# In the up product's first full pair: banks emptied first, the second pair's differences formed after

## The chip, the core and the metric

The kernel runs on one core of a Trainium2 chip. Five engines work beside each other, each through its own queue in order: TensorE (matmuls, PE in the profile, with its weight loads as PEld), VectorE (DVE), ScalarE (ACT), GpSimd (POOL) and SyncE (SP), which here issues nearly all DMAs. They wait for one another by semaphores. The metric is the device time of one execution in microseconds (us); lower is better. Three runs of the kernel before took 2182.22, 2184.85 and 2186.44 us, median 2184.85.

## What is computed

A decoder trunk of two layers over 1024 positions of width 1024, in float32. Each layer has a mixer (a gated one, then dilated attention) and behind it a dense MLP with a squared ReLU:

```python
for layer in range(DEPTH):
    y = _rms_norm(h, mix_norm_g[layer])
    ...
    h = h + y
    y = _rms_norm(h, mlp_norm_g[layer])
    h = h + jnp.square(jax.nn.relu(y @ w_up[layer])) @ w_down[layer]
return _rms_norm(h, final_norm_g)
```

`w_up` is 1024 x 4096 and `w_down` 4096 x 1024 in each layer. The change lies in the up product, `y @ w_up[layer]`, and so comes twice in a run.

## The kernel before

*Splits.* Every float32 operand of a matmul is split into an upper and a lower part (`split`, L207): ScalarE copies the source to a rounded type (L208), VectorE subtracts that copy from the source (L209). Three matmuls then make one product: upper by upper, upper by lower, lower by upper (`three`, L321).

*Up product by pairs.* The 4096 columns of `w_up` are taken as 16 pairs (q = 0 to 15) of two 128-column tiles; the 1024 positions are two halves. A pair is thus a 2 x 2 block of 128 x 512 results, c11, c21, c12, c22. Pairs 0 and 1 are computed plainly, with 8 products of 4 inputs, while the normed input is still being made. From pair 2 on, the first full pair, a block takes seven products instead of eight (a Strassen-Winograd form): `product` (L326) runs four inputs by three matmuls, 12 matmuls of 128x512, so a full pair has 84. Its order is 1, 5, 6, 7, then 2, 3, 4, the last three accumulated into banks that already hold something:

- bank `a`: product 1, copied by ScalarE to u (L705), later product 2 on top, giving c11
- bank `d`: product 5, copied by ScalarE to c22 (L717), later product 3 on top, for c12 (L745)
- bank `b`: product 6, added by VectorE to u (L727)
- bank `e`: product 7, added by VectorE to c22 (L733), later product 4 on top, for c21 (L750)

So TensorE may begin product 4 only when L733 has read bank e, product 3 when L717 has read bank d, product 2 when L705 has read bank a. L734 then adds u to c22. `squared` (L644) applies ReLU and the square on ScalarE (L646, L647).

*Differences.* The down product takes seven combinations of each pair's four results, so `hidden_terms` (L649) forms four differences on VectorE (L652, L653, L656, L658), and `kept` (L640, L642) stores the seven tiles to memory through SP's queue, 256 KB each. L652 and L658 write to one of two spare buffers, which come free when their stores have landed. Pair 1's differences are formed right after pair 1, as pair 2 begins on TensorE.

*Weights.* While pair q runs, the weights of pair q+1 are prepared: four raw tiles are loaded through SP (L169), GpSimd forms four combinations (L351, L352, L353, L356, in this order, the last three in place), and each of the seven is split. `steps` (L346) is a generator; every `more()` takes one step: the first splits 4 and issues the GpSimd steps 351 to 353, the second splits 1 and issues 356, then 5, 7, 6, 2, 3. In pair 2 the `more()` calls behind product 1 and 5 are placed after ScalarE's copies with `tc.issue_after`, which keeps an instruction of that engine behind a given one in its queue and adds no wait.

*Inputs.* `Terms` holds the inputs of the seven products, four tiles each. `rest` (L420) makes those of product 7 and the first three of product 4 as pair 1 ends; the fourth tile of product 4 is made by `last` (L427) within pair 2: a GpSimd copy (L430), then a split.

*What sets the order.* TensorE's order is the one written. On the other engines a scheduler lists the instructions by when it expects them ready, so the text's order is only a start; `tc.high_priority` and `tc.issue_after` bend it.

## Time and profile before

| | us |
|---|---|
| median of three runs | 2184.85 |
| the profiled execution | 2183.62 |
| its span, first to last instruction | 2180.8 |
| TensorE busy | 2141.2 (98%) |
| VectorE busy | 1548.9 (71%) |
| ScalarE busy | 1087.3 (50%) |
| GpSimd busy | 518.2 (24%) |

The mean granted clock of TensorE is 0.995 of full speed. A profile row of the timeline reads: start in us from the span's start, duration in us, engine, line, operation, output<-inputs by their names without numbers, shape, how many in a row, and in brackets the idle time of the engine before it with what ended it. A row of waits reads: who waited for whom, total us, times, longest. A row of stretches reads: from:to, length, busy time and count of PE, PEld, DVE, ACT and POOL, then the granted clock, the DMA engines' busy share and GB/s. "wp" is a split weight tile, "r" a raw weight tile, "t" a temporary, "b" a spare buffer, "mm" and "at" are PSUM banks, "hid" is the stored hidden tile, "keep" a kept input.

### The profile page before, as it was taken

To read this page: it belongs to the slowest core of one execution; us is meant where nothing else is said; L and a number is where in the kernel's file an instruction comes from. 1 tells how busy PE (TensorE), PEld (TensorE's weight loads), DVE (VectorE), ACT (ScalarE), POOL (GpSimd) and SP (SyncE) were. 2 spreads that over 40 slices of the span, in tenths; PEclk is the share of its full clock that TensorE was granted. 3 is DMA by queue.
4 is the path that set the end of the run, shared out by engine and by line. 5 is a ranking of instruction groups with operands and counts; after the bars stand their busy time and mean duration, and the time that the engine had idled before them with its cause. 6 is when DMAs were issued, how large, how long until landed. Compare 5 with 4: busy or idle time off the path is not lost.

```text
span 2180.8 us, 30391 instructions
## 1 busy us (share of the span) xinstructions
PE 2141.2 (98%) x10360; PEld 1776.6 (81%) x10360; DVE 1548.9 (71%) x2855; ACT 1087.3 (50%) x2200; POOL 518.2 (24%) x372
## 2 busy tenths in 40 slices
PE   9999999999999999999999999999999999999997
PEld 7888887888878888788888887887778888788886
DVE  7875278666688887771357676758976667988867
ACT  7644145555564443351356464656555556544432
POOL 2000224333324323510000000001433332332335
PEclk9999999999999999999999999999999999999999
DMA  6421104444355443333331322221154443554432
GB/s 213 133 70 49 39 27 161 159 156 151 119 181 186 145 151 107 106 123 129 121 76 54 83 56 55 75 55 30 39 179 157 147 155 123 190 169 147 150 91 98
DMA packets 167679, 253.88 MB, mean 116 GB/s; under 512 B 33641, under 2 KB 59364, under 8 KB 167524
## 3 DMA queue, kind: packets, MB, share of 16 engines
q1 hardware_dynamic: 166768, 250.71, 36.2%
q8 instruction: 81, 1.33, 0.3%
q10 hardware_dynamic: 756, 1.23, 0.2%
q14 instruction: 74, 0.61, 0.1%
HBM read 182.50 MB, written 69.37 MB: 115 GB/s over the span
## 4 chain that ended last, share of the span: by engine, by line
PE 78%; DVE 9%; DMA 5%; ACT 4%; issue 2%; POOL 1%; SPq 0%; DVEq 0%; ACTq 0%; POOLq 0%
PE at L180 39%; PE mm L180 37%; PE at L187 1%; DVE wp L209 1%; ACT t L1123 1%; DMA t<-bvec 1%; DMA t<-in_w_dl 1%; DVE y L209 1%; DMA r<-in_w_dn 1%; DMA sc<-st 1%; DVE N L1161 1%; DVE h L308 1%; DVE t L209 0%; DMA h<-in_xT 0%; DMA hr<-hid 0%
## 5 line engine op out<-in xcount | busy, mean ns | idle before, releaser
L208 ACT ACTIVATE wp<-r 128x512 fp32r<-128x512 f32 (+2 forms) x404 | 241.0, 600 | 358.4 <-PE at L180 237.4
L180 PE MATMUL at<-hx,wp 128*128 128x512 f32 x1770 | 413.3, 389 | 1.8 <-DVE h L817 1.7
L180 PE MATMUL mm<-y,whi 128*128 128x512 f32 x1312 | 412.3, 395 | 0.0
L180 PEld LDWEIGHTS at<-hx,wp 128*128 128x128 f32 x1770 | 332.0, 188 | 72.0 <-DVE h L817 3.0
L209 DVE TENSOR_TENSOR wp<-r,wp 128x512 fp32r<-128x512 f32 (+2 forms) x404 | 320.3, 801 | 70.0 <-ACT wp L208 66.4
L180 PE MATMUL at<-t,wp 128*128 128x512 f32 x1344 | 316.1, 391 | 6.3 <-DVE t L733 6.3
L180 PEld LDWEIGHTS at<-t,wp 128*128 128x128 f32 x1344 | 253.6, 189 | 60.0 <-DVE t L733 7.2
L264 POOL TENSOR_TENSOR t<-t 128x512 f32<-128x512 f32 (+1 forms) x66 | 83.6, 1267 | 859.1 <-ACT t L259 857.0
L180 PEld LDWEIGHTS mm<-y,whi 128*128 128x128 f32 x1312 | 240.8, 188 | 50.6
L180 PE MATMUL mm<-y,wlo 128*128 128x512 f32 x656 | 256.0, 390 | 0.0
L351 POOL TENSOR_TENSOR t<-r 128x512 f32<-128x512 f32 (+3 forms) x62 | 93.0, 1500 | 594.2 <-DMA r<-in_w_dn 191.8
L180 PE MATMUL mm<-y,wp 128*128 128x512 f32 x912 | 222.7, 390 | 0.4 <-DVE y L209 0.2
L180 PEld LDWEIGHTS mm<-y,wp 128*128 128x128 f32 x912 | 170.7, 188 | 37.4 <-issue 0.6
L180 PE MATMUL mm<-hx,wp 128*128 128x512 f32 x708 | 172.5, 390 | 2.4 <-DVE hx L209 1.2
L180 PEld LDWEIGHTS mm<-hx,wp 128*128 128x128 f32 x708 | 132.5, 188 | 31.8 <-DVE hx L209 2.0
L180 PEld LDWEIGHTS mm<-y,wlo 128*128 128x128 f32 x656 | 123.2, 188 | 26.6
L209 DVE TENSOR_TENSOR hx<-t,hx 128x512 fp32r<-128x512 f32 x192 | 142.7, 750 | 1.4 <-ACT hx L208 1.4
L817 DVE TENSOR_TENSOR h<-h,at 128x512 f32<-128x512 f32 x144 | 97.9, 682 | 47.7 <-PE at L180 45.7
L209 DVE TENSOR_TENSOR wlo<-r,whi 128x512 fp32r<-128x512 f32 x138 | 99.3, 737 | 41.3 <-ACT whi L208 34.1
L208 ACT ACTIVATE hx<-t 128x512 fp32r<-128x512 f32 x192 | 118.9, 629 | 17.6 <-DMA t<-hid 10.9
L208 ACT ACTIVATE whi<-r 128x512 fp32r<-128x512 f32 x138 | 84.1, 627 | 83.8 <-PE mm L180 54.4
L180 PE MATMUL at<-y,wp 128*128 128x512 f32 x480 | 119.0, 390 | 0.7 <-DVE wp L209 0.7
(199 smaller groups left out, 3211.7 us busy)
## 6 DMA issues: line engine op xcount, KB each, us to landing
t<-hid SPq DMA_DIRECT2D x182, 256.0 KB, 3.1
hid<-t SPq DMA_DIRECT2D x140, 256.0 KB, 2.3
r<-in_w_up SPq DMA_DIRECT2D x128, 256.0 KB, 2.7
r<-in_w_dn SPq DMA_DIRECT2D x88, 256.0 KB, 2.6
hid<-b SPq DMA_DIRECT2D x56, 256.0 KB, 2.1
r<-in_w_qkv SPq DMA_DIRECT2D x50, 256.0 KB, 2.6
r<-in_w_v SPq DMA_DIRECT2D x48, 256.0 KB, 3.1
vd<-vs SPq DMA_DIRECT2D x16, 512.0 KB, 3.9
```

The lines of the kernel that those rows point to most:

```text
L180: nc.tensor.matmul(out, lhsT, rhs, **kw)
L187: nc.tensor.transpose(out, src, ident)
L208: nc.scalar.activation(hi, src, AF.Copy)
L209: nc.vector.tensor_tensor(lo, src, hi.bitcast(F32), op=ALU.subtract)
L264: nc.gpsimd.tensor_tensor(self.acc, self.acc, sq, op=ALU.add)
L308: nc.vector.tensor_tensor(x, x, ps, op=ALU.add)
L351: tt(r3, r[0, 0], r[1, 0], op=ALU.subtract)
L817: return engine.tensor_tensor(hs[i, s], hs[i, s], src, op=ALU.add).ins
L1123: nc.scalar.activation(p[:, c], p[:, c], AF.Exp, bias=m, scale=-1.0, accum_out=dn)
L1161: nc.vector.tensor_tensor(o, o, pv[r, c], op=ALU.add)
```

## The change

```diff
         def last(self):
 
             t4 = temp()
             nc.gpsimd.tensor_copy(t4, self.kept[3][:, 1, :])
-            self.t[4].append(pair("t4").split(t4))
+            return lambda: self.t[4].append(pair("t4").split(t4))
...
+        def held_terms(q):
+            hidden_terms(q, c[q, 0, 0], c[q, 1, 0], c[q, 0, 1], c[q, 1, 1], c[q, 0, 0])
+
...
-                if s and i:
-                    hidden_terms(q, c[q, 0, 0], c[q, 1, 0], c[q, 0, 1], c[q, 1, 1], c[q, 0, 0])
+                if s and i and q == 0:
+                    held_terms(q)
...
             evacuated = nc.scalar.activation(c22, d, AF.Copy).ins
             if q == 2:
                 with tc.issue_after(evacuated):
+                    t4 = x.last()
                     more()
-                    x.last()
...
             b = at_bank()
             product(b, w[6], x.t[6])
-            more()
+            if q > 2:
+                more()
             nc.vector.tensor_tensor(u, u, b, op=ALU.add)
...
             e = at_bank()
             product(e, w[7], x.t[7])
-            more()
-            nc.vector.tensor_tensor(c22, c22, e, op=ALU.add)
+            if q > 2:
+                more()
+            emptied = nc.vector.tensor_tensor(c22, c22, e, op=ALU.add).ins
+            if q == 2:
+
+                with tc.issue_after(evacuated), tc.issue_after(emptied):
+                    t4()
+                    more()
+                    more()
+                    held_terms(1)
             nc.vector.tensor_tensor(c22, c22, u, op=ALU.add)
```

In pair 2 alone, the split of the fourth input tile of product 4, the splits of the next pair's weights 7 and 6, and pair 1's differences with their stores are written behind the addition that empties bank e (L733), and kept behind it in VectorE's queue; the splits among them are kept behind ScalarE's copy of bank d in ScalarE's queue as well. The GpSimd copy for that input tile stays where it was in the text. Pair 0's differences are formed as before. No instruction is added or taken away, and all other pairs are written as before. Line numbers in the prediction are those of the kernel before.

## The prediction

> **What bounds the kernel now.** I read the page first (busy shares and the chain that ended last), then TensorE's waits, then the stretches around the longest of them, then all engines there in order of time. Pairs are the loop's q: pairs 0 and 1 are plain products, pair 2 is the first full one.

> ```profile
> span 2180.8 us, 30391 instructions
> ...
> PE 78%; DVE 9%; DMA 5%; ACT 4%; issue 2%; POOL 1%; SPq 0%; DVEq 0%; ACTq 0%; POOLq 0%
> ```

> ```profile
> PE at L180 <- DVE t L733: 6.3, 2, 4.7
> ```

> ```profile
> 364.84 3.03 PE L180 MATMUL at<-t,wp 128*128 128x512 f32 x12 [1.58 <-DVE t L733]
> ```

> TensorE carries 78% of the chain, so only what makes it wait counts. Its largest wait, 6.3 us in two pieces, is for L733, the addition that empties bank e: twice in the program, once in each layer's MLP (1.58 us in layer 0, 4.74 in layer 1). The stretches price it. Each of the first four runs from product 5 of one full pair to product 5 of the next, and holds the same matmuls.

> ```profile
> 1600.30:1604.30 4.00, 3.96 (x9) 3.13 (x10) 2.48 (x4) 2.75 (x6) 0.00 (x0) 0.50 0.29 90
> ...
> 905.00:908.00 3.00, 3.00 (x7) 2.35 (x8) 3.00 (x6) 0.63 (x1) 1.18 (x2) 0.50 0.48 132
> ...
> 349.50:370.43 20.93, 19.35 (x85) 15.69 (x84) 17.29 (x21) 10.94 (x21) 7.25 (x5) 1.00 0.61 211
> 370.43:389.47 19.04, 19.04 (x85) 15.77 (x84) 15.97 (x20) 11.08 (x21) 7.92 (x6) 1.00 0.57 194
> 1581.84:1607.99 26.15, 21.41 (x85) 17.18 (x84) 22.06 (x29) 14.48 (x27) 8.36 (x6) 0.87 0.61 199
> 1607.99:1627.04 19.05, 19.05 (x86) 15.77 (x85) 14.65 (x18) 10.27 (x18) 8.30 (x6) 1.00 0.51 166
> ```

> The first number is the length, the one before the DMA share the granted clock. Pair 2 costs 20.93 - 19.04 = 1.89 us more than pair 3 in layer 0, and 26.15 - 19.05 = 7.10 us more in layer 1. The latter is a wait of 4.74 us (its row stands below) and 2.36 us of slow matmuls: the clock stood at 0.50 behind it. Together 8.99 us hang on this place. Here is why L733 came late in layer 1:

> ```profile
> 1587.85 0.68 DVE L209 TENSOR_TENSOR wp<-r,wp 128x512 fp32r<-128x512 f32 x1
> 1587.91 0.62 ACT L208 ACTIVATE wp<-r 128x512 fp32r<-128x512 f32 x1
> ...
> 1589.36 1.28 POOL L351 TENSOR_TENSOR t<-r 128x512 f32<-128x512 f32 x1 [7.78 <-DMA hid<-t]
> ...
> 1589.88 1.32 DVE L652 TENSOR_TENSOR b<-t 128x512 f32<-128x512 f32 x1 [1.35 <-DMA hid<-b]
> ...
> 1590.73 1.62 POOL L352 TENSOR_TENSOR r<-r 128x512 f32<-128x512 f32 x1
> 1591.12 1.77 DVE L209 TENSOR_TENSOR wp<-r,wp 128x512 fp32r<-128x512 f32 x1
> ...
> 1592.38 0.64 ACT L208 ACTIVATE wp<-r 128x512 fp32r<-128x512 f32 x1 [1.17 <-POOL r L352]
> 1592.42 1.62 POOL L353 TENSOR_TENSOR r<-r 128x512 f32<-128x512 f32 x1
> ...
> 1592.72 2.88 PE L180 MATMUL at<-y,wp 128*128 128x512 f32 x12
> 1592.82 1.78 DVE L653 TENSOR_TENSOR t<-t 128x512 f32<-128x512 f32 x1
> 1593.99 1.07 POOL L430 COPY t<-keep 128x512 f32<-128x512 f32 x1
> 1594.51 1.09 DVE L209 TENSOR_TENSOR wp<-r,wp 128x512 fp32r<-128x512 f32 x1
> ...
> 1595.03 1.71 POOL L356 TENSOR_TENSOR r<-r 128x512 f32<-128x512 f32 x1
> 1595.10 0.63 ACT L208 ACTIVATE t<-t 128x512 fp32r<-128x512 f32 x1 [2.09 <-POOL t L430]
> 1595.53 1.75 DVE L656 TENSOR_TENSOR t<-t 128x512 f32<-128x512 f32 x1
> ...
> 1597.21 0.68 DVE L209 TENSOR_TENSOR t<-t,t 128x512 fp32r<-128x512 f32 x1
> 1597.81 0.68 DVE L658 TENSOR_TENSOR b<-t 128x512 f32<-128x512 f32 x1
> 1598.41 0.68 DVE L209 TENSOR_TENSOR wp<-t,wp 128x512 fp32r<-128x512 f32 x1
> 1599.01 0.67 DVE L727 TENSOR_TENSOR t<-t,at 128x512 f32<-128x512 f32 x1
> 1599.61 0.68 DVE L733 TENSOR_TENSOR t<-t,at 128x512 f32<-128x512 f32 x1
> ...
> 1600.34 1.22 PE L180 MATMUL at<-t,wp 128*128 128x512 f32 x2 [4.74 <-DVE t L733]
> ```

> VectorE has no gap from 1589.88 on: nine instructions stand ahead of L733, four of them pair 1's differences (L652, L653, L656, L658). Four VectorE subtractions that run beside a POOL instruction take 1.09 to 1.78 us instead of 0.68, and end 0.56 us behind it (1592.82 + 1.78 = 1594.60 against POOL's 1592.42 + 1.62 = 1594.04); POOL's own 1.28 us becomes 1.62. TensorE would have begun product 4 when product 3 ends its 12 matmuls, at 1592.72 + 2.72 = 1595.44 (2.72 being the step between equal products, 19.04/7).

> **The change part by part.** Nothing is added or removed; instructions change places. In the order of the changed program's instructions VectorE has, behind the split at 1587.85: the splits of products 1 and 5's weights, L727, L733, the t4 split, the splits of weights 7 and 6, and only then pair 1's differences, threaded between pair 2's own work. On POOL the t4 copy (L430) moves behind L356. On SP the stores of pair 1's differences move behind two loads.

> *L733.* Weight 1's lower half can follow its upper half at 1587.91 + 0.62 = 1588.53 and end at 1589.2, ahead of POOL's first step (which waits for a store that nothing moves). POOL then runs unheld: 1590.73 + 1.28 = 1592.0. ScalarE's copy of weight 5 takes 0.64, to 1592.65; its subtraction waits out L353 (1592.1 to 1593.4) and ends 0.56 later, 1593.95. L727 and L733 follow in steps of 0.60 (1599.01 to 1599.61): bank e is empty at 1595.2, by 0.25 us in time. The other end: POOL's two steps at 1.62 as now, and 1.78 for each of weight 5's split (from 1593.02), L727 and L733: 1598.2, a wait of 2.8 us. The near end holds, since an addition that reads a bank isn't slowed beside POOL:

> ```profile
> 378.27 0.67 DVE L727 TENSOR_TENSOR t<-t,at 128x512 f32<-128x512 f32 x1
> ```

> ```profile
> 377.88 1.63 POOL L356 TENSOR_TENSOR r<-r 128x512 f32<-128x512 f32 x1 [1.29 <-issue]
> ```

> *t4.* POOL: L356 starts behind weight 5's split, 1593.95 + 1.28 = 1595.2, the copy 1.07 to 1596.3; ScalarE 0.63 to 1596.95, VectorE to 1597.6. Product 4 needs that tile's lower half at its 11th matmul, 1595.44 + 10 x 0.227 = 1597.7. On the edge; with 1.71 for L356, 0.3 us late. I put 0.2 us for L733 and t4 together.

> *What is late next.* Behind the t4 split on VectorE stand ten instructions (weights 7, 6 and 2, L652, L734, L653, L656, L745, L658, weight 3) at 0.60 each, to 1603.6, then pair 2's L652 to 1604.3. SP issues seven stores, the last of them that of this L652, before the third load for pair 4, which feeds L351 and L352:

> ```profile
> 1603.63 0.38 SPq L169 DMA_DIRECT2D r<-in_w_up  x1
> ```

> ```profile
> 1618.88 2.88 PE L180 MATMUL at<-y,wp 128*128 128x512 f32 x12
> ...
> 1621.60 2.88 PE L180 MATMUL at<-t,wp 128*128 128x512 f32 x12
> ```

> ```profile
> r<-in_w_up SPq DMA_DIRECT2D x128, 256.0 KB, 2.7
> ```

> ```profile
> 350.00:355.00 5.00, 5.00 (x24) 4.14 (x23) 3.86 (x6) 3.19 (x6) 1.17 (x1) 1.00 1.00 360
> ```

> That load goes out at 1604.7, 1.1 us later than now, while TensorE comes 7.1 us earlier. Landed after 2.7 us: 1607.4; L351 to 1608.7, L352 (1.62) to 1610.4, ScalarE's weight 5 to 1611.0 and, behind it in ScalarE's queue, pair 3's copy of bank d (0.6) to 1611.6. TensorE needs that copy at product 3, 1618.88 - 7.10 = 1611.78: just in time. L733 of pair 3 stands behind weight 5's subtraction (L353 ends about 1611.8, so 1612.4), L727 and weight 7's (held by L356), and ends near 1615.0 against 1621.60 - 7.10 = 1614.50: 0.5 us. At the full DMA rate of 360 GB/s one 256 KB transfer takes 0.73 us; two stores ahead of the load make it land 1.5 us later, and the wait 2.0 us. The ends are 0 and 2.0; I take 0.5, as the stores are issued about as fast as they drain.

> *Layer 0* has more room.

> ```profile
> 353.83 1.28 POOL L351 TENSOR_TENSOR t<-r 128x512 f32<-128x512 f32 x1 [7.49 <-DMA hid<-t]
> ```

> POOL's L351 comes 353.83 - 349.50 = 4.33 us behind product 5, in layer 1 7.52: every time above has 3.19 us more there, so no wait is left, and the 1.89 us go.

> The sum: -8.99 + 0.2 + 0.5 = -8.3 us. The profiled execution took 2183.62 us (2.8 around its span): 2175.3. The three runs lie at 2182.22 to 2186.44, median 2184.85, from which it would be 2176.5. I predict 2176.0, between the two.

> ```profile
> 904.96 1.56 PE L180 MATMUL mm<-hx,y 128*128 128x512 f32 x3 [2.26 <-DVE b L836]
> ```

> What a leftover wait costs beyond its length: the clock was 0.50 from 905 to 908 (a stretch shown above), right behind this wait of 2.26 us, while the 1.58 us that layer 0 now waits left the clock of its stretch at 1.00. So I charge a wait above some 2 us with 1.5 us more (3 us at half speed). [...]

> **The rivals.**

> *A: the wait shrinks but stays in layer 1's pair 2.* If POOL's and VectorE's blocked durations hold throughout, bank e is empty at 1598.2: 2.8 us of wait and 1.5 of clock come back, with 0.5 later: -8.99 + 4.8 = -4.2, 2180. For: ScalarE's and POOL's steps are chained to a landing store. Against: VectorE is idle from 1589.2 to 1592.65 and no longer holds POOL up.

> *B: the loads of pair 4 come too late; slower.* Place: the third load behind seven stores, in both layers. If it lands x us after 1607.5, layer 1 waits x + 0.5, and layer 0 x - 3.2; above 2 us each pays 1.5 for the clock. At x = 5.1 that is 7.1 + 1.9 = 9.0: all is given back. 5.1 us are seven stores of 0.73, so that is the case of all seven standing in the queues when the load is issued. At x = 6.5, with pair 4's fourth load behind five more stores, it is 8.5 + 4.8 = 13.3, 4.3 above now: 2188. Against: VectorE makes the stores 0.6 us apart or more, so most have drained.

> *C: no change.* The scheduler's order moves a bank's emptying, but the wait only changes its releaser (t4's chain over POOL, 3 us longer than worked): 2183.6. Against: the rows of that chain above.

> **How the numbers follow.** Forecast 0.70 (2173 to 2178.5), A 0.13, C 0.09, B 0.08. The low end is the fastest run less all of 8.99, 2173; the high end, 2181, takes in A. Under 0.2% (4.4 us) this kernel's measurement can't tell from no change: that is 2180.5 to 2189.2. Faster gets the forecast and most of A, 0.81; same takes C and the rest of A, 0.12; slower, from B, 0.07.

> **What would show it.** TensorE's waits: no L733 wait above 0.5 us; both pair-2 stretches at 19.0 to 19.8 us; no clock of 0.50 near 1600. On VectorE L733 ends about 4.4 us earlier after product 5 in layer 1, behind only the three weight splits. L652 to L658 of pair 1 appear in pair 2's second half. Wrong would be: product 4 of pair 2 waiting for the t4 split, or pair 3 waiting more than 2 us, with SP's third load landing after 1609 (on the old clock).

## The result, and the profile after

The changed kernel takes 2176.12 us (median of five runs, 2174.14 to 2177.02) against 2186.44 (five runs, 2182.22 to 2187.48) of the kernel before: a ratio of 0.996, 95% interval 0.995 to 0.9971. In a second comparison it took 2174.65 (five runs, 2172.84 to 2175.51) against 2183.32 (21 runs), ratio 0.996 (0.9947 to 0.9974). The gain is 10.3 us in the first, 8.7 in the second. The profiled execution took 2177.02.

In the changed kernel's lines L705 is L709, L717 is L721, L727 is L732, L733 is L739, L734 is L747, L745 is L758. First its page, the span and the chain's shares:

```profile
span 2174.9 us, 30386 instructions
...
PE 80%; DVE 8%; DMA 5%; ACT 4%; issue 2%; POOL 1%; SPq 1%; DVEq 0%; ACTq 0%; POOLq 0%
```

Then its longest waits of TensorE (who waited for whom, total us, times, longest):

```profile
PE at L187 <- DVE rq L247: 3.4, 3, 2.4
PE mm L180 <- DVE h L308: 3.2, 3, 2.0
```

The wait for the emptying of bank e, 6.3 us and the longest before, has left the list; the two at its head stand at lines that the change doesn't touch. The stretches from product 5 of pair 2 to that of pair 3, and on to pair 4's, in layer 0 (first two rows) and layer 1:

```profile
349.84:368.88 19.04, 19.04 (x85) 15.77 (x84) 13.85 (x22) 11.46 (x22) 6.05 (x5) 1.00 0.60 211
368.88:387.92 19.04, 19.04 (x85) 15.77 (x84) 13.41 (x19) 9.81 (x18) 5.95 (x5) 1.00 0.57 191
1581.04:1600.08 19.04, 19.04 (x85) 15.77 (x84) 14.18 (x23) 11.85 (x23) 6.05 (x5) 1.00 0.52 171
1600.08:1619.45 19.37, 19.37 (x85) 15.69 (x84) 14.01 (x20) 11.52 (x21) 5.84 (x4) 1.00 0.64 216
```

Pair 2 went from 20.93 to 19.04 in layer 0 and from 26.15 to 19.04 in layer 1, at full clock; pair 3 of layer 1 gave back 19.37 - 19.05 = 0.32. So these two places give 1.89 + 7.11 - 0.32 = 8.68 us. All engines in layer 1's pair 2, in order of time:

```profile
1591.31 0.63 ACT L208 ACTIVATE wp<-r 128x512 fp32r<-128x512 f32 x1 [0.87 <-POOL r L352]
1591.36 1.29 POOL L353 TENSOR_TENSOR r<-r 128x512 f32<-128x512 f32 x1
...
1591.98 1.22 DVE L209 TENSOR_TENSOR wp<-r,wp 128x512 fp32r<-128x512 f32 x1 [3.51 <-ACT wp L208]
1592.73 1.63 POOL L356 TENSOR_TENSOR r<-r 128x512 f32<-128x512 f32 x1
1593.12 0.68 DVE L732 TENSOR_TENSOR t<-t,at 128x512 f32<-128x512 f32 x1
...
1593.72 0.67 DVE L739 TENSOR_TENSOR t<-t,at 128x512 f32<-128x512 f32 x1
1594.30 0.61 POOL L430 COPY t<-keep 128x512 f32<-128x512 f32 x1
1594.64 2.88 PE L180 MATMUL at<-t,wp 128*128 128x512 f32 x12
1594.94 0.63 ACT L208 ACTIVATE t<-t 128x512 fp32r<-128x512 f32 x1 [3.00 <-POOL t L430]
1595.61 0.69 DVE L209 TENSOR_TENSOR t<-t,t 128x512 fp32r<-128x512 f32 x1 [1.22 <-ACT t L208]
...
1598.62 0.69 DVE L653 TENSOR_TENSOR t<-t 128x512 f32<-128x512 f32 x1
```

VectorE now idles 3.51 us, then makes weight 5's lower half, L732 and L739 in a row: bank e is empty at 1593.72 + 0.67 = 1594.39, and product 4 starts at 1594.64 with no wait. Pair 1's L653 stands in the second half, where GpSimd has nothing to do, and takes 0.69 us instead of 1.78.

### The profile page after: what moved, and what is told of

It is laid out like the page before. It is cut to its first block, busy times and chain, and to the rows that moved or that the text cites. A ratio compares the mean times of both kernels' runs of the same rounds, so it can differ in the third digit from the quotient of the medians.

```text
span 2174.9 us, 30386 instructions
## 1 busy us (share of the span) xinstructions
PE 2139.6 (98%) x10360; PEld 1774.5 (82%) x10360; DVE 1541.6 (71%) x2855; ACT 1086.5 (50%) x2200; POOL 514.3 (24%) x372
## 4 chain that ended last, share of the span: by engine, by line
PE 80%; DVE 8%; DMA 5%; ACT 4%; issue 2%; POOL 1%; SPq 1%; DVEq 0%; ACTq 0%; POOLq 0%
PE at L180 40%; PE mm L180 39%; PE at L187 1%; DMA t<-bvec 1%; ACT t L1136 1%; DVE wp L209 1%; DMA sc<-st 1%; DMA h<-in_xT 1%; DMA r<-in_w_dn 1%; DMA t<-in_w_dl 1%; DVE N L1174 1%; DMA hr<-hid 1%; DVE h L308 0%; DVE h L830 0%; DVE wlo L209 0%
## 5 line engine op out<-in xcount | busy, mean ns | idle before, releaser
L208 ACT ACTIVATE wp<-r 128x512 fp32r<-128x512 f32 (+2 forms) x404 | 240.9, 600 | 356.4 <-PE at L180 229.0
L180 PE MATMUL at<-hx,wp 128*128 128x512 f32 x1770 | 412.9, 389 | 1.7 <-DVE h L830 1.7
L180 PE MATMUL mm<-y,whi 128*128 128x512 f32 x1312 | 412.4, 395 | 0.0
L180 PEld LDWEIGHTS at<-hx,wp 128*128 128x128 f32 x1770 | 332.0, 188 | 71.7 <-DVE h L830 2.6
L209 DVE TENSOR_TENSOR wp<-r,wp 128x512 fp32r<-128x512 f32 (+2 forms) x404 | 323.5, 808 | 77.2 <-ACT wp L208 73.7
L180 PE MATMUL at<-t,wp 128*128 128x512 f32 x1344 | 313.9, 389 | 0.0
L180 PEld LDWEIGHTS at<-t,wp 128*128 128x128 f32 x1344 | 252.2, 188 | 52.8 <-DVE t L739 0.4
L180 PEld LDWEIGHTS mm<-y,whi 128*128 128x128 f32 x1312 | 240.7, 188 | 50.6
L180 PE MATMUL mm<-y,wlo 128*128 128x512 f32 x656 | 256.0, 390 | 0.0
L351 POOL TENSOR_TENSOR t<-r 128x512 f32<-128x512 f32 (+3 forms) x62 | 92.7, 1494 | 596.6 <-DMA r<-in_w_up 194.1
L180 PE MATMUL mm<-y,wp 128*128 128x512 f32 x912 | 222.7, 390 | 0.4 <-DVE y L209 0.2
L180 PEld LDWEIGHTS mm<-y,wp 128*128 128x128 f32 x912 | 170.7, 188 | 37.4 <-issue 0.6
L180 PE MATMUL mm<-hx,wp 128*128 128x512 f32 x708 | 172.6, 390 | 3.2 <-DVE hx L209 1.6
L180 PEld LDWEIGHTS mm<-hx,wp 128*128 128x128 f32 x708 | 132.4, 188 | 32.9 <-DVE hx L209 2.5
L180 PEld LDWEIGHTS mm<-y,wlo 128*128 128x128 f32 x656 | 123.1, 188 | 26.8
L209 DVE TENSOR_TENSOR hx<-t,hx 128x512 fp32r<-128x512 f32 x192 | 141.1, 741 | 1.9 <-ACT hx L208 1.9
L208 ACT ACTIVATE hx<-t 128x512 fp32r<-128x512 f32 x192 | 119.0, 630 | 17.8 <-DMA t<-hid 13.7
L209 DVE TENSOR_TENSOR wlo<-r,whi 128x512 fp32r<-128x512 f32 x138 | 98.9, 735 | 40.8 <-ACT whi L208 35.6
L208 ACT ACTIVATE whi<-r 128x512 fp32r<-128x512 f32 x138 | 84.0, 627 | 84.4 <-PE mm L180 54.3
L180 PE MATMUL at<-y,wp 128*128 128x512 f32 x480 | 119.0, 390 | 0.7 <-DVE wp L209 0.7
## 6 DMA issues: line engine op xcount, KB each, us to landing
t<-hid SPq DMA_DIRECT2D x182, 256.0 KB, 3.2
hid<-t SPq DMA_DIRECT2D x140, 256.0 KB, 2.3
r<-in_w_up SPq DMA_DIRECT2D x128, 256.0 KB, 2.7
r<-in_w_dn SPq DMA_DIRECT2D x88, 256.0 KB, 2.6
hid<-b SPq DMA_DIRECT2D x56, 256.0 KB, 2.2
r<-in_w_qkv SPq DMA_DIRECT2D x50, 256.0 KB, 2.6
r<-in_w_v SPq DMA_DIRECT2D x48, 256.0 KB, 3.5
```

Of the source, the lines that this page charges most:

```text
L180: nc.tensor.matmul(out, lhsT, rhs, **kw)
L208: nc.scalar.activation(hi, src, AF.Copy)
L209: nc.vector.tensor_tensor(lo, src, hi.bitcast(F32), op=ALU.subtract)
L351: tt(r3, r[0, 0], r[1, 0], op=ALU.subtract)
```

## The experiments

Each starts from the changed kernel; lines shift by a few. "Product 4" and the banks are those of the front; the t4 split is that of the fourth input tile of product 4. Experiments 1 to 3 were timed once each, and 21 single runs of the kernel before lie between 2179.40 and 2187.66 us: what these three show is read from their stretches, not from their times.

**1. The differences alone.** Only pair 1's differences stay behind bank e; the t4 split and the splits of weights 7 and 6 go back to their old places.

```diff
-            return lambda: self.t[4].append(pair("t4").split(t4))
+            self.t[4].append(pair("t4").split(t4))
...
-                    t4 = x.last()
                     more()
+                    x.last()
...
-            if q > 2:
-                more()
+            more()
...
-            if q > 2:
-                more()
+            more()
...
-                    t4()
-                    more()
-                    more()
                     held_terms(1)
```

> Only pair 1's differences are moved behind the emptying of bank e; the t4 split and the splits of weights 7 and 6 stand where they stood before, so VectorE's order is weight 5, the addition from bank b, t4 split, weight 7's split, the addition that empties bank e. Theory (each instruction ahead of that addition costs its place in VectorE's queue, and the t4 split can't start before GpSimd's copy): in the changed kernel the t4 split ran 1595.61 to 1596.30 and weight 7's 1596.22 to 1596.91; the addition would follow to 1597.5 against product 4's place at 1594.64, so TensorE waits 2.9 us in layer 1, with 1.5 to 2.4 us of halved clock behind it: the stretch from product 5 of pair 2 to product 5 of pair 3 takes 23.4 to 24.4 us instead of 19.04. In layer 0, with 2.75 us more room, 0.1 to 0.3 us: 19.1 to 19.4. Rival (the differences are the whole of it, and the splits' place is of no matter): both stretches at 19.04, as in the changed kernel.

2181.59 us, the kernel before beside it 2183.13 (one run each). Waits, stretches (pair 2 of layer 0, then layer 1) and VectorE's rows of layer 1:

```profile
PE at L180 <- DVE t L737: 3.3, 1, 3.3
```

```profile
349.67:368.76 19.09, 19.09 (x85) 15.69 (x84) 13.37 (x21) 10.33 (x19) 6.03 (x5) 1.00 0.55 200
1580.78:1605.03 24.25, 20.94 (x85) 16.84 (x84) 18.03 (x28) 14.70 (x27) 6.42 (x6) 0.93 0.57 195
```

```profile
1593.43 0.67 DVE L731 TENSOR_TENSOR t<-t,at 128x512 f32<-128x512 f32 x1
...
1595.90 0.69 DVE L209 TENSOR_TENSOR t<-t,t 128x512 fp32r<-128x512 f32 x1 [1.80 <-ACT t L208]
...
1597.11 0.68 DVE L737 TENSOR_TENSOR t<-t,at 128x512 f32<-128x512 f32 x1
```

The theory had 23.4 to 24.4 us for layer 1's pair 2 and 19.1 to 19.4 for layer 0's, and 24.25 and 19.09 came; its rival (the differences are all there is, 19.04) falls. With the differences gone, bank b is emptied at 1593.43 (L731), but the t4 split stands ahead of L737 in VectorE's queue, waits 1.80 us for ScalarE, and L737 waits behind it. In layer 0 that is hidden (19.09); in layer 1, 5.2 of the 7.1 us above 19.04 stay.

**2. The splits alone.** The other half: the t4 split and those of weights 7 and 6 stay behind bank e, the differences go back.

```diff
-                if s and i and q == 0:
+                if s and i:
                     held_terms(q)
...
-                    held_terms(1)
```

> Only the t4 split and the splits of weights 7 and 6 are moved behind the emptying of bank e; pair 1's differences stay ahead of it. Theory (place in VectorE's queue): two instructions of 0.60 us less stand ahead than in the kernel before, so the waits of 4.74 and 1.58 us become 3.5 and 0.4: stretches of pair 2 of 24.1 to 25.2 us in layer 1 (3.5 of wait and 1.5 to 2.4 of clock) and 19.4 in layer 0. Rival (the splits, with the t4 copy ahead of them on GpSimd, are the whole of it): both at 19.0 to 19.4.

2179.43 us against 2183.13 (one run each). Waits, stretches and VectorE's rows of layer 1:

```profile
PE at L180 <- DVE t L739: 3.9, 2, 3.7
```

```profile
348.37:367.96 19.59, 19.33 (x85) 15.68 (x84) 16.99 (x21) 10.30 (x19) 7.25 (x5) 1.00 0.63 218
1579.62:1604.22 24.60, 20.95 (x85) 16.83 (x84) 20.98 (x27) 14.37 (x27) 8.35 (x6) 0.93 0.59 203
```

```profile
1593.43 1.75 DVE L656 TENSOR_TENSOR t<-t 128x512 f32<-128x512 f32 x1
...
1596.31 0.68 DVE L739 TENSOR_TENSOR t<-t,at 128x512 f32<-128x512 f32 x1
```

In layer 1 it came as the theory had it (24.1 to 25.2), in layer 0 0.2 us longer than its 19.4: the slowed differences are back ahead of the emptying, and 5.6 us stay in layer 1. There the halves alone give 26.15 - 24.25 = 1.9 and 26.15 - 24.60 = 1.6 us, about a quarter each of the 7.1: either one left ahead of L739 keeps it late, and only both together free it. In layer 0, which had less to lose, the differences alone give 20.93 - 19.09 = 1.84 us of the 1.89 and the splits alone 20.93 - 19.59 = 1.34.

**3. The t4 copy four times over**, to make that chain late by a known amount.

```diff
             t4 = temp()
-            nc.gpsimd.tensor_copy(t4, self.kept[3][:, 1, :])
+            for _ in range(4):
+                nc.gpsimd.tensor_copy(t4, self.kept[3][:, 1, :])
```

> The changed kernel with GpSimd's copy of the t4 tile done four times into the same buffer; nothing else differs, and VectorE's order is the same. The three more copies take 3 x 0.65 us = 1.95 us. Theory (the t4 split was 0.6 us early in layer 1: ended 1596.30, needed by the 11th matmul of product 4 at 1594.64 + 2.27 = 1596.91; 3.4 us early in layer 0): product 4 of pair 2 waits 1.3 us in layer 1, between its 10th and 11th matmul, without loss of clock (under 2 us), and pair 3 loses 0.3 to 1.2 us, as VectorE's queue behind the t4 split is 1.95 us later: stretches 20.3 for pair 2 and 19.4 to 20.3 for pair 3. In layer 0 no wait, 19.04. Rival (the t4 split is not near the edge: the time from GpSimd's copy to product 4 has slack): 19.04 for pair 2 in both layers.

2179.03 us against 2183.13 (one run each). The stretches of pairs 2 and 3 in layer 0, then in layer 1, and TensorE in layer 1:

```profile
349.51:368.55 19.04, 19.04 (x85) 15.78 (x84) 12.08 (x19) 9.75 (x19) 7.89 (x8) 1.00 0.50 168
368.55:388.49 19.94, 19.80 (x85) 15.54 (x84) 13.18 (x19) 10.67 (x20) 5.84 (x4) 1.00 0.62 199
1581.84:1602.14 20.30, 19.58 (x86) 15.70 (x84) 13.71 (x22) 11.38 (x22) 8.04 (x8) 1.00 0.45 154
1602.14:1622.10 19.96, 19.82 (x86) 15.54 (x84) 14.44 (x21) 11.93 (x22) 5.83 (x4) 1.00 0.64 215
```

```profile
1598.13 0.50 PE L180 MATMUL at<-t,wp 128*128 128x512 f32 x1 [0.49 <-ACT t L208]
1598.86 0.72 PE L180 MATMUL at<-t,wp 128*128 128x512 f32 x2 [0.23 <-DVE t L209]
```

Layer 1's pair 2 came as worked out, 20.30. GpSimd's copies took 2.63 us in place of 0.61. Of these 2.02 us, 20.30 - 19.04 = 1.26 reach TensorE, which now waits within product 4 for t4's two halves: the chain had some 0.76 us to spare. The miss is pair 3 of layer 0, 19.94 where 19.04 was expected, from SP's and ScalarE's rows:

```profile
371.23 0.45 SPq L169 DMA_DIRECT2D r<-in_w_up  x1
```

```profile
375.56 0.63 ACT L208 ACTIVATE wp<-r 128x512 fp32r<-128x512 f32 x1 [2.80 <-DMA r<-in_w_up]
...
379.21 0.58 ACT L722 ACTIVATE t<-at 128x512 f32<-128x512 f32 x1
```

The third load of the next pair went out 371.23 - 368.55 = 2.68 us after product 5 and was in use 4.33 us later; in the changed kernel's layer 0 it was 0.74 us (369.62 - 368.88) and 3.02 (to 372.64). So the chain is 1.94 + 1.31 = 3.25 us later here. The expectation had the queue 1.95 us later and nothing for the landing; why the load took longer to land stays open.

**4 and 5. One layer alone.** The new order in layer 0 only (4) and in layer 1 only (5); the edit of 4, with `layer == 0` and `layer != 0` exchanged for those of layer 1 in 5:

```diff
-                if s and i and q == 0:
+                if s and i and (q == 0 or layer != 0):
                     held_terms(q)
...
-                    t4 = x.last()
+                    if layer == 0:
+                        t4 = x.last()
                     more()
+                    if layer != 0:
+                        x.last()()
...
-            if q > 2:
+            if q > 2 or layer != 0:
                 more()
...
-            if q > 2:
+            if q > 2 or layer != 0:
                 more()
...
-            if q == 2:
+            if q == 2 and layer == 0:
```

> The change in layer 0's MLP alone. Theory (the two places add up): pair 2's stretch 19.04 us in layer 0 and some 26 us in layer 1; about 1.9 us faster than before, ratio 0.9991, which five rounds hardly tell from no change. Rival (the gain is somewhere else, or layer 0's share is what the clock makes of it): no change at all, or more than 4 us.

> The change in layer 1's MLP alone. Theory: pair 2's stretch 19.04 in layer 1, 20.9 in layer 0; 7.1 less 0.33 for pair 3, 6.8 us faster, ratio 0.9969. Rival (the extra gain over the 8.7 us of the two places, seen in the medians of the changed kernel, sits in layer 1): 8.5 us or more.

Medians of 11 runs each, beside 2183.32 of the kernel before: layer 0 alone 2181.72, ratio 0.9994 (0.9985 to 1.0002); layer 1 alone 2177.61, ratio 0.9972 (0.9964 to 0.9981). Pair 2 in both layers, of 4 and then of 5:

```profile
349.54:368.58 19.04, 19.04 (x85) 15.77 (x84) 14.31 (x23) 11.59 (x22) 6.12 (x5) 1.00 0.63 214
1578.58:1604.33 25.75, 20.77 (x85) 16.75 (x84) 21.40 (x28) 14.48 (x27) 7.83 (x6) 0.93 0.59 196
```

```profile
349.02:370.04 21.02, 19.34 (x86) 15.69 (x84) 17.31 (x21) 10.94 (x21) 7.24 (x5) 1.00 0.61 208
1581.33:1600.37 19.04, 19.04 (x85) 15.77 (x84) 14.20 (x23) 11.88 (x23) 6.07 (x5) 1.00 0.51 171
```

Each layer's stretch falls to 19.04 where the new order stands and stays near its old length where it doesn't (25.75 against 26.15, 21.02 against 20.93: such a wait varies by some tenths of a us). The medians fall by 1.6 and 5.7 us, where 1.9 and 6.8 were expected; for layer 0 alone the interval holds no change too, so its 1.9 us are shown by the stretch, not by the time. For layer 1 alone it runs from 4.1 to 7.9 us, which holds the 6.8 and not the 8.5 of the rival.

**6. The third load earlier.** Pair 4's weights are requested at high priority, to take the load away from behind the seven stores.

```diff
-            wn = down.weights(0) if down else up_weights(q + 1)
+            with tc.high_priority(offset=PRIO) if q == 3 else nullcontext():
+                wn = down.weights(0) if down else up_weights(q + 1)
```

> The changed kernel, with the loads of pair 4's raw weights at a raised priority, which moves the third of them ahead of five of the seven stores on SP. Theory (pair 3 in layer 1 lost 0.33 us because that load was late for GpSimd's first step, which held ScalarE's copy of bank d): the load goes out near 1599.8 instead of 1603.57, GpSimd's first step starts before 1604 instead of after 1606, and pair 3's stretch is 19.05 instead of 19.37; in time 0.3 us, not to be told from the changed kernel. Rival (VectorE's queue itself is late in pair 3): still 19.3 or more.

2174.69 us (five runs), ratio to before 0.9959 (0.9947 to 0.9972). Pair 3 of layer 1, and GpSimd's first step there:

```profile
1599.64:1618.68 19.04, 19.04 (x85) 15.77 (x84) 16.00 (x22) 12.05 (x22) 6.15 (x4) 1.00 0.70 235
```

```profile
1602.64 1.30 POOL L351 TENSOR_TENSOR t<-r 128x512 f32<-128x512 f32 x1 [8.40 <-DVE b L652]
```

The load goes out behind two stores instead of seven, L351 begins 3.0 us after pair 3's product 5 (1599.64) instead of 6.5 (1606.56 - 1600.08 in the changed kernel), and the pair has no wait left.

**7. The changed kernel again**, beside the runs of 4 to 6.

> The changed kernel once more, beside the others on this chip. Theory (8.99 us less 0.33 at the two places, all else noise): 8.7 us faster than the kernel before, ratio 0.9960. Rival (the 10.3 us between the medians are real and part of it comes from elsewhere): 10 us or more, with stretches outside the two places that are shorter in both profiles of the changed kernel than before.

2174.65 us: the 10.3 us of the first comparison are not repeated, and 8.67 is near what the places add up to (8.68 by the first profile's stretches, 9.00 - 0.04 = 8.96 with this run's pair 3). The interval is 5.7 to 11.6 us, so an agreement to a hundredth is luck. Its pair 3 of layer 1:

```profile
1599.21:1618.30 19.09, 19.09 (x86) 15.71 (x84) 13.63 (x20) 11.19 (x20) 5.81 (x4) 1.00 0.64 215
```

Against 19.04 it lost 0.05 us there, not 0.33, so experiment 6 has nothing left to win, and its time is the same.

## Why the prediction was right

2176.0 was predicted, 2176.12 and 2174.65 were measured. That the first lies within 0.12 us is luck: the kernel before stood at 2186.44 beside it, above both bases of the prediction (2183.62 and 2184.85), and the gain was 10.3 us, not 8.3. The second comparison, with 21 runs of the kernel before and a gain of 8.7, is the fairer test. The steps, one by one:

*8.99 us hang on this place.* Shown by the stretches: pair 2's two lost 9.00 us together, clock included, and each layer's lost its own share when that layer alone was changed (experiments 4, 5).

*L733 (now L739) lies 0.25 us in time.* The prediction's 13.4 us from product 5 to the empty bank (1595.2 - 1581.84) came out at 13.35 (1594.39 - 1581.04), and product 4 began 0.25 us later. (Among the signs to look for, the prediction has L733 some 4.4 us earlier after product 5; its own rows give 1600.29 - 1595.2 = 5.1, and 18.45 - 13.35 = 5.1 came. And the rows that it shows have five slowed subtractions, not four.) The step that mattered was that the additions that read a bank weren't slowed beside GpSimd: L732 and L739 took 0.68 and 0.67, although L356 ran until 1592.73 + 1.63 = 1594.36, while weight 5's subtraction, between two tiles of SBUF, took 1.22 and ended 0.55 us behind L353. Rival A, which had all of them slowed, falls with these rows.

*t4 on the edge, 0.2 us.* It was better: the copy took 0.61 us, not the 1.07 taken from before, where L653, a subtraction between two SBUF tiles, ran beside it until 1594.60; now L739, which reads a bank, was all that did. The lower half was there at 1595.61 + 0.69 = 1596.30, 0.6 us ahead of the 11th matmul (1594.64 + 2.27); experiment 3 gives 0.76 from the other side. The first 0.2 us of the sum was therefore nothing. That t4 could have decided (rival C's mechanism) is true of the place: with the chain 2.02 us later TensorE waits for it.

*0.5 us in pair 3.* The mechanism was right, the size 0.33 and 0.05 us (above 19.04) in the two profiles of the changed kernel. The changed kernel's first profile: SP, then ScalarE, then TensorE's weight loads.

```profile
1598.13 0.33 SPq L642 DMA_DIRECT2D hid<-b  x1
1599.34 2.25 SPq L642 DMA_DIRECT2D hid<-t  x4
1601.74 1.77 SPq L642 DMA_DIRECT2D hid<-b  x2
1603.57 0.44 SPq L169 DMA_DIRECT2D r<-in_w_up  x1
```

```profile
1606.48 0.63 ACT L208 ACTIVATE wp<-r 128x512 fp32r<-128x512 f32 x1 [1.38 <-DMA r<-in_w_up]
...
1610.12 0.58 ACT L721 ACTIVATE t<-at 128x512 f32<-128x512 f32 x1
```

```profile
PEld at L180 <- DVE t L739: 0.4, 1, 0.4
```

The load goes out behind seven stores, 3.49 us after product 5 of pair 3 (3.8 predicted), bank d is copied by 1610.70, 0.26 us ahead of product 3 (1600.08 + 4 x 2.72), and the wait is for L739. Counted from the pair's product 5, the prediction had that copy's end at 10.7 us (1611.6 - 1600.88), with 10.9 allowed. The traces give, for its end and the length of the pair, 7.2 us and 19.04 (experiment 6), 10.4 and 19.09 (7), 10.6 and 19.37 (the first profile), 10.8 and 19.53 (experiment 5), 11.2 and 19.94, 11.3 and 19.96 (experiment 3's layers): from some 10.3 us on, what is late is paid for in full. So B's mechanism is real, but cost half a us at most with the order of the change and 0.9 with its chain made later; the 2 us above which B added a clock charge were not reached.

*Layer 0 has 3.19 us more room.* 2.75 it is (L351 came 7.58 us behind product 5 in layer 1, 4.83 in layer 0); enough, pairs 2 and 3 there are both at 19.04.

*The sum.* The terms should have been -8.99 + 0.05 to 0.33, so -8.7 to -8.9 instead of -8.3; the second comparison has -8.67. The first profiled span fell by less, 5.9 us, because other places moved, which the last section shows in part.

## What to carry to other kernels

A bank's emptying is worth as much as what stands ahead of it in its engine's queue: list those instructions, their producers and their durations beside GpSimd (here up to 1.78 us instead of 0.68), and move behind it all that isn't needed earlier, since each half of the move alone gave a quarter of the layer-1 gain. Then follow what the moved work holds up one stage later: here stores that pushed a load back, which cost 0.05 to 0.5 us, and 0.9 once the moved work itself came 2 us later, because the chain behind that load ends close to when it is needed. Price the place by the whole stretch between equal points, clock included, since the wait alone (4.74 of 7.10 us) undercounts it.

## What the runs showed of the hardware

Whether a wait of some 2 us halves the clock isn't fixed by its length. The prediction charged 1.5 us above about 2 us. One place shows otherwise. In the changed kernel's first profile, TensorE's row that ends a wait (in brackets) and the stretch behind it:

```profile
1509.45 0.73 PE L180 MATMUL mm<-o,whi 128*128 128x512 f32 x2 [1.96 <-DVE h L308]
```

```profile
1510.60:1514.00 3.40, 3.40 (x10) 2.62 (x9) 3.27 (x4) 1.92 (x4) 2.90 (x2) 0.50 0.00 0
```

The same in the kernel before:

```profile
1510.87 0.73 PE L180 MATMUL mm<-o,whi 128*128 128x512 f32 x2 [1.95 <-DVE h L308]
```

```profile
1510.90:1514.30 3.40, 3.40 (x15) 2.82 (x16) 3.37 (x5) 2.03 (x4) 2.01 (x2) 1.00 0.00 0
```

The granted clock is the third number from the end: after 1.96 us it was 0.50, after 1.95 us 1.00. The changed kernel ran 10 matmuls there in the time of the 15 before, 1.1 us lost in work that the change doesn't touch; another 0.5 went to a wait in layer 1's down product (1.41 us against 0.92). That is more than half of the 2.8 us by which the first profiled span fell short of 8.68; the rest stays open. The wait in the down product is no accident of one run: it takes 1.41 to 1.81 us in the five profiles with the whole new order in layer 1, and 0.92 to 1.15 in the other four. What links it to the change stays open. At the place of 905 us that the prediction showed, where 2.26 us had halved the clock, 2.35 us lowered it to 0.50 in the first profile of the changed kernel (from 903.05 to 906.46), and 2.23 left it at 1.00 in the second.

```profile
1507.21:1510.62 3.41, 1.45 (x8) 1.03 (x7) 3.31 (x7) 1.19 (x2) 0.00 (x0) 1.00 0.22 77
```

The wait of 1.95 us before (1508.92 to 1510.87) is cut by a window's edge, and TensorE is busy for 2.56 and 1.74 us in the two windows that share it:

```profile
1505.78:1509.19 3.41, 2.56 (x12) 1.92 (x12) 3.28 (x6) 1.61 (x4) 0.00 (x0) 1.00 0.62 181
1509.19:1512.60 3.41, 1.74 (x8) 1.43 (x9) 3.35 (x6) 1.73 (x3) 0.39 (x1) 1.00 0.13 49
```

Over these two profiles, leaving out the first 20 and the last 15 us, four windows at full clock were idle for 57 to 69% (from 901.62 and 1594.52 before, from 899.64 and 1507.21 in the changed kernel), and each was followed by a fall; of the others, idle for 49% or less, none was. So a window idle for 57% was enough here; it needn't be idle whole, and between the waits of 1.96 and 1.95 us the place in the grid is what differed. No run moved a wait on purpose to try it.
